# Two modulation sections of layer 1, loaded and multiplied around the low-rank projections of layer 0

## The chip, the cores and the metric

The kernel runs on one core of a Trainium2 chip. The metric is the device time of one execution in microseconds; the time of the kernel before is the median of three runs. Half of a per cent is 5.3 us. A core has TensorE (matrix products, its weight loads overlap them), VectorE (DVE), ScalarE (ACT), GpSimd (POOL) and SyncE (SP), which here issues nearly all weight loads. All inputs lie in HBM, weights as fp32.

## The reference

Two layers of a diffusion trunk over 256 latent tokens (`x`) and 256 context tokens (`xc`), 1024 wide. Each layer derives six modulation rows for either stream from a conditioning vector, with one large weight, mixes tokens, and sends every token to two of 32 experts:

```python
ada = silu(c) @ w_ada[l] + b_ada[l]             # the same for c_ctx; w_ada[l]: 1024 x 6144
sh1, sc1, g1, sh2, sc2, g2 = split(ada, 6)      # sections 0 .. 5
h = x * (1 + sc1) + sh1
p = h @ w_in[l]                                 # q low-rank 384 | kv low-rank 256 + 32 | conv 512 | pool 256
...                                             # latent attention, convolution, pooling, one out projection
x = layer_norm(ALPHA * x + g1 * mix, ln1)
h2 = x * (1 + sc2) + sh2
x = layer_norm(ALPHA * x + g2 * moe(h2), ln2)   # router, then 32 experts of 1024 x 256
```

The modulation of a layer depends on `c` and `c_ctx` alone, so it can be computed at any time before its layer.

## The kernel before

**Loads.** All large weights come through one list, `plan`, in pieces of at most 1 MB. `pump` gives the next piece of the list to the slot that was freed first and issues its load on SP's queue; `done` frees a piece's slot once its last reader has read it. Until layer 0's experts there are six slots (`RING`), so piece n of the list waits until piece n - 6 is used up. Section `sec` of layer `l` is four pieces of 1 MB (`ada_src`); `ink_src` are the two pieces of the weights for kv low-rank and rotary key (called k here), `inq_src` the two of q low-rank, then `ukv` and `uq` (two). The list for layer 0 is: section 1, two column blocks, section 0, one column block, section 2, k, q, ukv, uq, sections 3 to 5, out projection (four), then **sections 1 and 0 of layer 1**, then the experts.

**Modulation.** `ada_mm` (L296) multiplies one piece: 8 matmuls of 32 columns by 256, four side by side in the array; the profile counts each twice, 64 for a section. `ada_add` (L305, L307) copies or adds the result into a row tile on VectorE.

**Mixing of layer 0.** After the column blocks come section 2 and then `lowrank` for k and for q: the weights of two of the eight row blocks (a chunk) are split into a high half (ScalarE, L395) and a remainder (VectorE or POOL, L401) and multiplied with the tokens in three products (L407 to L409, `mm3`). A fixed list gives the first k chunk's remainder to POOL. There are two buffers for split weights. VectorE also runs the taps of a depthwise convolution (L606), which are needed only later. Then follow keys, values and queries from ukv and uq, attention head by head (with the products of sections 3 to 5 between heads), and the out projection.

**Router.** For each of four blocks of 128 tokens: normalise, transpose on TensorE (L1068), copy (ScalarE, L1073), product with the router weights (L1079), result to VectorE (L1081). `fill_ada(n)` multiplies n of the eight pieces of layer 1's sections 1 and 0 between these, by the list `FILL[0]`: 0, 1, 2 and 2 behind the blocks and 6 at the end. Then short VectorE steps choose experts and places; a one-hot product gathers the tokens, and a conditional block for overfull experts follows (L1592). The residual for the next norm is scaled and shifted by rows that are broadcast from HBM (loads L344, POOL L1490, then L1470 and L1471 on VectorE and POOL).

**Experts.** 16 pairs: gate and up products (L1400), the hidden values on VectorE (L1409, L1410), transpose (L1416), down product (L1444) and scatter (L1458). Five more 1 MB slots are free here.

**Order.** Outside the experts, where TensorE's order is as written, a scheduler orders each engine's instructions with a model of their times; what is written first goes first when its inputs are there by that model. On the chip each engine then runs its list in that order.

Of the kernel before, what the change touches and what calls it, by code (L numbers as in the profile page):

```python
# [26 lines left out]
CAP = 64  # L27
NONE = 1024.0
RING = 6
FILL = ((0, 1, 2, 2, 6), (0, 1, 3))  # L30
PA = (0, 1)
VP = (5, 7, 9)
SPG = ((4, 7, 18, 20), (2, 4, 6, 10, 12, 14, 20))
# [14 lines left out]
def trunk(ctx: ExitStack, tc: tile.TileContext, a, out, dbg=None, cap=CAP):  # L48
# [14 lines left out]
    def ada_src(l, sec):  # L63
        w = a["w_ada"][l, :, sec * D:(sec + 1) * D].rearrange("(p j) c -> p j c", j=8)
        for jp in range(4):
            plan.append((("ada", l, sec, jp), w[:, 2 * jp:2 * jp + 2, :], (2, D)))

    def in_src(l, which=(0, 1, 2)):
        w = a["w_in"][l].rearrange("(p j) c -> p j c", j=8)
        for k in which:  # L70
            n, c0 = "agp"[k], (672, 928, 1184)[k]
            plan.append(((n, l), w[:, :, c0:c0 + 256], (8, 256)))

    def inq_src(l):
        w = a["w_in"][l].rearrange("(p j) c -> p j c", j=8)
        for h in range(2):
            plan.append((("q", l, h), w[:, 4 * h:4 * h + 4, 0:384], (4, 384)))

    def ink_src(l):
        w = a["w_in"][l].rearrange("(p j) c -> p j c", j=8)  # L80
        for h in range(2):
            plan.append((("k", l, h), w[:, 4 * h:4 * h + 4, 384:672], (4, 288)))

    def uq_src(l):
        w = a["uq"][l].rearrange("(p j) c -> p j c", j=3)
        for h in range(2):
            plan.append((("uq", l, h), w[:, :, 512 * h:512 * h + 512], (3, 512)))

    def ukv_src(l):
        plan.append((("ukv", l), a["w_ukv"][l].rearrange("(p j) c -> p j c", j=2), (2, 1024)))  # L90

    def out_src(l):
        w = a["w_out"][l].rearrange("(b p) c -> p b c", p=128)
        for hf in range(2):
            for bb in (1, 0):
                plan.append((("out", l, hf, bb), w[:, 4 * bb:4 * bb + 4, 512 * hf:512 * hf + 512], (4, 512)))
# [9 lines left out]
    def exp_src(l):  # L106
        def piece(nm, key, pick):
            plan.append(((nm,) + key, lambda: expert(nm, l, pick), (2, 1024)))

        def pair(nm, i):  # L110
            for e in (2 * i, 2 * i + 1):
                piece(nm, (l, e), lambda w, e=e: w[e:e + 1])

        def picked(nm):
            piece(nm, ("v",), lambda w: w[ds(extra[0], 1)])

        pair("g0", 0)
        for i in range(E // 2):
            pair("g1", i)
            if i + 1 < E // 2:  # L120
                pair("g0", i + 1)
            if i + 2 < E // 2 or (i + 2 == E // 2 and not AHEAD[l]):
                pair("wd", i)
            elif i + 1 == E // 2:
                if AHEAD[l]:
                    pair("wd", i - 1)
                for hf in range(2):
                    n = CUT[l][hf]
                    plan.append((("wd", l, 2 * i + hf), lambda hf=hf, i=i, n=n: [
                        a["w_down"][l, e:e + 1, :, c:c + n].rearrange("o (p j) c -> p (o j) c", j=2)  # L130
                        for c in range(512 * hf, 512 * hf + 512, n) for e in (2 * i, 2 * i + 1)],
                        (1024 // n, 2 * n)))
            if l == L - 1 and i == VP[1]:
                picked("g0")
                picked("g1")
            if l == L - 1 and i == VP[2]:
                picked("wd")

    for l in range(L):
        if l == 0:  # L140
            ada_src(0, 1)
            in_src(0, (0, 1))
            ada_src(0, 0)
            in_src(0, (2,))
        else:
            ada_src(1, 2)
            in_src(1, (0, 1))
            ada_src(1, 3)
            in_src(1, (2,))
        if l == 0:  # L150
            ada_src(0, 2)
        ink_src(l)
        inq_src(l)
        ukv_src(l)
        uq_src(l)
        for key in ((0, 3), (0, 4), (0, 5)) if l == 0 else ((1, 4),):
            ada_src(*key)
        out_src(l)
        for sec in (1, 0) if l == 0 else (5,):
            ada_src(1, sec)  # L160
        exp_src(l)

    if dbg is not None:
# [125 lines left out]
    def ada_mm(l, sec, ps, j0, j1):  # L289
        k = PLACE[sec][1]  # L290
        for jq in range(j0, j1):
            w = get(("ada", l, sec, jq))
            for jj in range(2):
                j = 2 * jq + jj
                for q in range(4):
                    T.matmul(ps[32 * q:32 * q + 32, :256], scw[:, j, 6 - 2 * k:38 - 2 * k],  # L296
                             w[:, jj, q * 256:q * 256 + 256], start=(j == 0), stop=(j == 7),
                             skip_group_check=True, tile_position=(0, 32 * q))
            done(("ada", l, sec, jq))
# [9 lines left out]
    def ada(l, sec, psum):  # L309
        ps = psum()  # L310
        ada_mm(l, sec, ps, 0, 4)
        ada_add(l, sec, ps)
# [54 lines left out]
    def mixing(l, P, norm):  # L367
# [3 lines left out]
        with ExitStack() as cs:  # L371
# [290 lines left out]
            if l:  # L662
                ada_mm(1, 3, ps3, A3, 4)
                ada_add(1, 3, ps3)
            else:
                ada(0, 2, psum)


            def lowrank(nm, toks, width, pss, n0=0, n1=4):
                for n in range(n0, n1):  # L670
                    hh, jq = divmod(n, 2)
                    w = get((nm, l, hh))
                    wh, wl = wsplit(w[:, 2 * jq:2 * jq + 2, :], 2 * width)
                    if jq:
                        done((nm, l, hh))
                    for jj in range(2):
                        j = 4 * hh + 2 * jq + jj
                        for k, t in enumerate(toks):
                            mm3(pss[k][:, :width], hTh[j][:, t * 128:(t + 1) * 128],
                                hTl[j][:, t * 128:(t + 1) * 128], wh[:, jj, :], wl[:, jj, :],  # L680
                                j == 0, j == 7)
                return pss
# [44 lines left out]
            with tc.issue_after(kept_pow[0].ins):  # L727
                conv_part(1, CONV1[l], CONV[l])
            lowrank("q", range(nq), 384, pq_, QS[l], 4)
            cos, sn = rope[:, :, 0:32], rope[:, :, 32:64]  # L730
            tr = t2(FT)[:, 0:128].rearrange("p (a b c) -> p a b c", a=2, b=2)
            kv_ = kr[:, 0:2, :].rearrange("p t (x y r) -> p t x y r", x=2, y=2)
# [317 lines left out]
            lg = per.tile([128, 4, 36], FT, tag="lg", name="lg")  # L1050
            mvs, hTs = [], {}

            todo = [(1, s_, j) for s_ in ((1, 0) if l == 0 else (5,)) for j in range(4)]
            held = {}

            def fill_ada(n):
# [44 lines left out]
            def behind(t):  # L1101

                if t >= 1:
                    merge(t - 1, 1)
                    rows_T(t - 1)
                    stats(t - 1)
                    fill_ada(FILL[l][t - 1])
                if t >= 2:
# [13 lines left out]
            else:  # L1122
# [4 lines left out]
                for t in range(nq):  # L1127
                    fill_ada(FILL[l][t])
                    if t + 1 < nq:
# [26 lines left out]

            fill_ada(FILL[l][-1])
            for t in range(nq):
# [805 lines left out]
```

## Time and profile before

| | |
|---|---|
| median of three runs (1063.36 to 1068.73) | 1065.06 us |
| the profiled execution, its own time | 1073.01 us |
| its span, first to last instruction | 1071.4 us |
| mean granted clock of TensorE | 0.943 |
| TensorE busy | 946.6 us (88%) |
| VectorE busy | 621.0 us (58%) |
| moved by DMA | 305.41 MB, mean 285 GB/s |

The rows of the page and of the trace's views come from the one profiled execution. Times in them are in us from the span's start. In a list in order of time a row has the start, the duration, the engine, the line, the operation, result and inputs, shapes and the number of instructions that are merged; in brackets stands the engine's idle time before it and what ended it. In a row of a stretch each engine has its busy time and, in parentheses, its instructions; the last three numbers are TensorE's granted clock as a share of full speed, the mean busy share of the 16 DMA engines, and GB/s.

### The profile page before, as it was taken

What the parts mean: (1) busy time and instruction counts of PE and PEld (TensorE: products, weight loads), DVE (VectorE), ACT (ScalarE), POOL (GpSimd) and SP (SyncE); (2) the same over time, 40 slices, a digit from 0 to 9 for tenths busy, and PEclk for the clock granted to TensorE, in tenths of its full rate; (3) what the DMA queues carried; (4) which work ended last, traced back from release to release, by engine and by line L of the source; (5) the groups of instructions that cost most, each with busy time, mean ns of one, the idle gap of its engine ahead of it and who ended that gap; (6) DMA issues with size and microseconds to landing.
All of it is one profiled execution on the core that took longest, in us unless ns stands there. A gap on an engine that the chain in (4) does not pass through costs nothing. (4 is left out here: it accounts for less than half of the span.)

```text
span 1071.4 us, 14154 instructions
## 1 busy us (share of the span) xinstructions
PE 946.6 (88%) x5217; PEld 561.0 (52%) x5217; DVE 621.0 (58%) x1169; ACT 312.6 (29%) x614; POOL 327.0 (31%) x284
## 2 busy tenths in 40 slices
PE   4995899999687999999999888988958997999994
PEld 3675786688452445444444587745733443444442
DVE  3499967757854344364333899877572343334336
ACT  2443455632401111111111445543312221222211
POOL 2346520001462333333424533102061222123222
PEclk9896999999888999999999999999769998999997
DMA  9843225866898999999998667356677999999981
GB/s 353 329 148 115 97 81 195 318 150 201 310 329 290 289 401 402 403 390 371 401 385 330 246 227 241 137 208 209 237 240 275 390 380 405 380 399 394 401 302 41
DMA packets 95530, 305.41 MB, mean 285 GB/s; under 512 B 10247, under 2 KB 30727, under 8 KB 87392
## 3 DMA queue, kind: packets, MB, share of 16 engines
q1 hardware_dynamic: 89744, 293.77, 75.1%
q0 software_dynamic: 4272, 6.14, 1.8%
q10 hardware_dynamic: 1440, 4.54, 1.1%
q8 instruction: 43, 0.70, 0.3%
q14 instruction: 31, 0.25, 0.1%
HBM read 309.03 MB, written 4.72 MB: 293 GB/s over the span
## 5 line engine op out<-in xcount | busy, mean ns | idle before, releaser
L1462 POOL TENSOR_TENSOR x<-x,tm 128x512 f32<-128x512 f32 x96 | 122.8, 1297 | 306.0 <-DVE tm L1461 305.6
L1400 PE MATMUL gu<-ring,xt 128*64 128x512 f32 x504 | 171.7, 626 | 0.0
L1400 PE MATMUL gu<-slot,xt 128*64 128x512 f32 x416 | 132.3, 605 | 0.0
L1435 DVE SCALAR_TENSOR_TENSOR O<-d,iw,O 128x512 fp32r<-128x512 f32 x63 | 47.2, 750 | 121.3 <-ACT O L1434 121.2
L1458 PE MATMUL y<-O,gt 128*128 128x512 f32 (+2 forms) x400 | 108.6, 407 | 4.2 <-DVE tm L1461 3.4
L1458 PEld LDWEIGHTS y<-O,gt 128*128 128x128 f32 (+1 forms) x400 | 69.6, 188 | 51.1 <-issue 25.9
L1461 DVE TENSOR_TENSOR tm<-y,lnb 128x512 f32<-128x512 f32 (+1 forms) x102 | 68.7, 677 | 45.8 <-PE y L1458 44.2
L1400 PEld LDWEIGHTS gu<-ring,xt 128*64 128x64 f32 x504 | 49.4, 143 | 67.3 <-issue 63.2
L1444 PE MATMUL d<-ring,ht 128*64 128x512 f32 x264 | 82.7, 597 | 1.0 <-DMA ring<-in_w_down_dram 1.0
L1434 ACT ACTIVATE O<-d,iw 128x512 fp32r<-128x512 f32 x63 | 43.3, 688 | 137.5 <-PE d L1444 136.5
L395 ACT ACTIVATE w<-ring 128x1024 fp32r<-128x1024 f32 (+2 forms) x50 | 47.3, 945 | 97.1 <-PE p L409 73.7
L606 DVE SCALAR_TENSOR_TENSOR c0b<-c0a,hw,c0b 128x256 f32<-128x256 f32 (+1 forms) x105 | 72.8, 739 | 0.5
L1409 DVE SCALAR_TENSOR_TENSOR hd<-th,gu 128x256 f32<-128x256 f32 x32 | 13.5, 421 | 89.3 <-ACT th L1408 89.3
L1400 PEld LDWEIGHTS gu<-slot,xt 128*64 128x64 f32 x416 | 38.3, 139 | 50.1 <-issue 47.6
L401 DVE TENSOR_TENSOR w<-ring,w 128x1024 fp32r<-128x1024 f32 (+2 forms) x40 | 50.2, 1256 | 22.9 <-ACT w L395 22.7
L408 PE MATMUL p<-w,hT 128*128 128x288 f32 (+1 forms) x112 | 39.8, 356 | 18.0 <-DVE w L401 17.9
L1444 PE MATMUL d<-slot,ht 128*64 128x512 f32 x168 | 52.6, 595 | 0.0
L1359 POOL DMA_INDIRECT xg<-h2d,ix x28 | 32.9, 1175 | 51.8 <-DVE ix L1358 23.1
L296 PE MATMUL p<-ring,scw 128*32 128x256 f32 x672 | 44.5, 399 | 1.9 <-DMA ring<-in_w_ada_dram 1.9
L1408 ACT ACTIVATE th<-gu 128x256 f32<-128x256 f32 x32 | 12.3, 385 | 108.9 <-PE gu L1400 108.9
L408 PE MATMUL p<-w,mix 128*128 128x512 f32 x96 | 38.5, 401 | 4.7 <-DVE w L401 4.7
L1444 PEld LDWEIGHTS d<-ring,ht 128*64 128x64 f32 x264 | 24.2, 137 | 34.9 <-issue 32.0
(429 smaller groups left out, 1932.6 us busy)
## 6 DMA issues: line engine op xcount, KB each, us to landing
ring<-in_w_ada_dram SPq DMA_DIRECT2D x46, 1024.0 KB
ring<-in_w_down_dram SPq DMA_DIRECT2D x32, 1024.0 KB
ring<-in_w_gate_dram SPq DMA_DIRECT2D x63, 512.0 KB
ring<-in_w_up_dram SPq DMA_DIRECT2D x63, 512.0 KB
slot<-in_w_gate_dram SPq DMA_DIRECT2D x54, 512.0 KB
slot<-in_w_up_dram SPq DMA_DIRECT2D x54, 512.0 KB
slot<-in_w_down_dram SPq DMA_DIRECT2D x21, 1024.0 KB
ring<-in_w_in_dram SPq DMA_DIRECT2D x6, 1024.0 KB
```

The source lines that it names most:

```text
L296: T.matmul(ps[32 * q:32 * q + 32, :256], scw[:, j, 6 - 2 * k:38 - 2 * k], w[:, jj, q * 256:q * 256 + 256], start=(j == 0), stop=(j == 7), ...
L395: kept_hi.append(S.activation(h_, src, AF.Copy))
L401: ins = e.tensor_tensor(l_, src, h_.bitcast(FT), op=OP.subtract)
L408: T.matmul(ps, lh, rl, start=False, stop=False, skip_group_check=True)
L606: V.scalar_tensor_tensor(acc, tap(b, k), hw[:, b, k:k + 1], acc, op0=OP.mult, op1=OP.add)
L1400: T.matmul(gu[64 * s:64 * s + 64, :].rearrange("p (g c) -> p g c", g=2), xt[h][:, j % 4, o0 + 64 * s:o0 + 64 * s + 64], ws[s].rearrange("p ...
L1434: S.activation(oh, ps, AF.Copy, scale=w)
L1435: V.scalar_tensor_tensor(ol, ps, w, oh.bitcast(FT), op0=OP.mult, op1=OP.subtract)
L1444: T.matmul(ps[64 * s:64 * s + 64, :n], ht[:, k, 64 * s:64 * s + 64], ws(s, k, c, n), start=(k == 0), stop=(k == 1), skip_group_check=True, ...
L1458: T.matmul(ps, GT[key][r, t * 128:(t + 1) * 128], O[key][k][r, c], start=(i == 0 and k == 0), stop=(i == m - 1 and k == 1))
L1461: V.tensor_tensor(tm, ps, gates[t // 2][hf][:, c0:c0 + n], op=OP.mult)
L1462: eng.tensor_tensor(x[:, t, cols], x[:, t, cols], tm, op=OP.add)
```

## The change

The four pieces of section 1 of layer 1 move in the list from behind the out projection to between section 2 of layer 0 and k; those of section 0 to between q and ukv. Their products are written where section 2's are, ahead of the k projection, and behind the q projection. Nothing is left to fill in during layer 0's router: the list `todo` is empty there, and `FILL[0]` is all zeros. Layer 1 keeps its own.

```diff
--- before.py
+++ after.py
@@ -27,7 +27,7 @@
 CAP = 64
 NONE = 1024.0
 RING = 6
-FILL = ((0, 1, 2, 2, 6), (0, 1, 3))
+FILL = ((0, 0, 0, 0, 0), (0, 1, 3))
 PA = (0, 1)
 VP = (5, 7, 9)
 SPG = ((4, 7, 18, 20), (2, 4, 6, 10, 12, 14, 20))
@@ -149,15 +149,18 @@
             in_src(1, (2,))
         if l == 0:
             ada_src(0, 2)
+            ada_src(1, 1)
         ink_src(l)
         inq_src(l)
+        if l == 0:
+            ada_src(1, 0)
         ukv_src(l)
         uq_src(l)
         for key in ((0, 3), (0, 4), (0, 5)) if l == 0 else ((1, 4),):
             ada_src(*key)
         out_src(l)
-        for sec in (1, 0) if l == 0 else (5,):
-            ada_src(1, sec)
+        if l:
+            ada_src(1, 5)
         exp_src(l)
 
     if dbg is not None:
@@ -664,6 +667,7 @@
                 ada_add(1, 3, ps3)
             else:
                 ada(0, 2, psum)
+                ada(1, 1, psum)
 
 
             def lowrank(nm, toks, width, pss, n0=0, n1=4):
@@ -727,6 +731,8 @@
             with tc.issue_after(kept_pow[0].ins):
                 conv_part(1, CONV1[l], CONV[l])
             lowrank("q", range(nq), 384, pq_, QS[l], 4)
+            if l == 0:
+                ada(1, 0, psum)
             cos, sn = rope[:, :, 0:32], rope[:, :, 32:64]
             tr = t2(FT)[:, 0:128].rearrange("p (a b c) -> p a b c", a=2, b=2)
             kv_ = kr[:, 0:2, :].rearrange("p t (x y r) -> p t x y r", x=2, y=2)
@@ -1050,7 +1056,7 @@
             lg = per.tile([128, 4, 36], FT, tag="lg", name="lg")
             mvs, hTs = [], {}
 
-            todo = [(1, s_, j) for s_ in ((1, 0) if l == 0 else (5,)) for j in range(4)]
+            todo = [(1, 5, j) for j in range(4 * l)]
             held = {}
 
             def fill_ada(n):
```

## Rows read from the trace of the kernel before

**Rows 1.** 40 slices of the page, 26.8 us each: TensorE busy, GB/s moved

```profile
PE   4995899999687999999999888988958997999994
...
GB/s 353 329 148 115 97 81 195 318 150 201 310 329 290 289 401 402 403 390 371 401 385 330 246 227 241 137 208 209 237 240 275 390 380 405 380 399 394 401 302 41
```

**Rows 2.** busy time by stretch: engine columns, granted clock, DMA share, GB/s

```profile
80.00:90.00 10.00, 3.14 (x16) 2.90 (x15) 10.00 (x7) 3.86 (x6) 9.69 (x7) 0.65 0.57 215
...
150.00:160.00 10.00, 10.00 (x49) 8.29 (x48) 6.18 (x17) 3.96 (x7) 3.49 (x3) 1.00 0.30 106
```

**Rows 3.** TensorE in order of time: start, duration, line; idle before, releaser

```profile
73.37 3.66 PE L296 MATMUL p<-ring,scw 128*32 128x256 f32 x64
...
87.40 0.61 PE L408 MATMUL p<-w,hT 128*128 128x288 f32 x1 [6.86 <-DVE w L401]
...
98.84 0.61 PE L408 MATMUL p<-w,hT 128*128 128x288 f32 x1 [5.41 <-DVE w L401]
...
134.61 0.73 PE L780 MATMUL p<-t,w 128*128 128x512 f32 x2 [1.21 <-DVE w L401]
```

**Rows 4.** who SP's queue waited for until 420: total, times, longest

```profile
SPq L187 <- PE gu L1400: 21.1, 3, 12.3
```

**Rows 5.** TensorE's waits in the experts of layer 0: total, times, longest

```profile
PE y L1416 <- DMA ring<-in_w_up_dram: 1.3, 1, 1.3
PE d L1444 <- DMA ring<-in_w_down_dram: 1.0, 1, 1.0
```

**Rows 6.** TensorE in order of time, at the end of layer 0's router

```profile
279.08 1.93 PE L296 MATMUL p<-ring,scw 128*32 128x256 f32 x32
280.95 1.98 PE L1079 MATMUL p<-wb,hT 128*128 128x36 f32 x16
```

**Rows 7.** VectorE in order of time, router and first expert pair

```profile
282.96 0.20 DVE L1081 TENSOR_TENSOR lg<-p,sums 128x36 f32<-128x36 f32 x1 [0.97 <-PE p L1079]
...
309.16 1.23 DVE L1343 TENSOR_SCALAR gt<-iot,iw 128x512 fp32r<-128x512 f32 x1
...
310.64 0.48 DVE L1343 TENSOR_SCALAR gt<-iot,iw 128x512 fp32r<-128x512 f32 x1
...
316.53 1.21 DVE L1471 TENSOR_TENSOR x<-x,lnb 128x1024 f32<-128x1024 f32 x1
...
320.08 5.88 DVE L1471 TENSOR_TENSOR x<-x,lnb 128x1024 f32<-128x1024 f32 x1
```

**Rows 8.** ScalarE in order of time, the last token block of the router

```profile
278.61 1.07 ACT L1073 ACTIVATE hT<-p 128x512 f32<-128x512 f32 x2
```

**Rows 9.** SP's DMA issues before the experts of layer 0

```profile
292.51 1.60 SPq L344 DMA_DIRECT2D lnb<-in_rpack_dram  x2
```

**Rows 10.** SP's DMA issues in order of time, around the low-rank projections

```profile
54.68 21.02 SPq L189 DMA_DIRECT2D ring<-in_w_in_dram  x4
76.23 0.34 SPq L189 DMA_DIRECT2D ring<-in_w_ukv_dram  x1
```

**Rows 11.** TensorE's clock and the DMAs' GB/s: idle, then busy again

```profile
80.60:83.00 2.40, 0.00 (x0) 0.99 1.00 406
...
87.40:93.40 6.00, 6.00 (x24) 0.52 0.40 131
```

**Rows 12.** one 1 MB piece alone on the queues (issued at 104.18)

```profile
104.00:109.00 5.00, 4.92 (x34) 4.54 (x33) 4.94 (x9) 4.56 (x16) 0.00 (x0) 1.00 0.60 210
```

**Rows 13.** POOL and ScalarE in order of time: the two halves of a split

```profile
71.90 1.88 POOL L401 TENSOR_TENSOR w<-ring,w 128x576 fp32r<-128x576 f32 x1
...
74.78 0.68 ACT L395 ACTIVATE w<-ring 128x576 fp32r<-128x576 f32 x1
```

**Rows 14.** VectorE in order of time, between the first splits

```profile
85.53 1.81 DVE L401 TENSOR_TENSOR w<-ring,w 128x576 fp32r<-128x576 f32 x1
...
96.98 1.81 DVE L401 TENSOR_TENSOR w<-ring,w 128x576 fp32r<-128x576 f32 x1
```

**Rows 15.** TensorE in order of time, router products of layer 1

```profile
767.13 7.04 PE L1079 MATMUL p<-wb,hT 128*128 128x36 f32 x32
```

## The prediction

> **What bounds the kernel now.** I read the page's 40 slices first, then busy time by stretch where the change takes away and where it adds, then the engines in order of time there. The slices show three stages for layer 0 [rows 1]: token mixing (to about 265 us), the router (to about 295), the experts (to about 590). Within mixing there are two kinds of time. In slices 4 and 5 the DMAs move 97 and 81 GB/s, because the ring is full and its pieces wait to be consumed; this is where the change wants to load. From 80 to 90 us VectorE is busy for all of 10.00 us and TensorE for 3.14; from 150 to 160 it is the other way round, TensorE is full and VectorE has 6.18 [rows 2]. So the low-rank projections (77 to 131 us) wait for VectorE, which runs convolution taps between the weight splits, while everything behind them, to the end of the out projection, is bound by TensorE. What is added to TensorE is free only where it falls in one of the holes before the full stretch: 6.86 us ahead of the second chunk of the k weights, 5.41 us ahead of the third, and 1.21 us ahead of the first key product, each released by a split on VectorE [rows 3].
>
> The moved pieces now stand in front of the expert weights, and the DMAs move about 330 GB/s in slices 10 to 12 [rows 1]. That looks like a bottleneck relieved, but two rows say that it isn't the one which counts. Before the experts get going, SP's queue once waits 12.3 us for TensorE to free a weight buffer [rows 4]: all buffers are full by then, in either kernel. And after that TensorE waits for expert weights 1.3 and 1.0 us in all [rows 5]. Full sooner is still full.
>
> **What is taken away at the router.** Eight pieces of 1 MB and their 64 matmuls, which the profile counts as 128. One section costs 3.66 us [rows 3]. Nearly all of it lies beside other work: the chain there goes over normalisation, transposes, router products and then short VectorE steps. One fill is on the path: 1.93 us of it stands in front of the last token block's router products, and VectorE waits for them until 282.96 [rows 6, 7]. Their input is ready when ScalarE ends its copies, at 278.61 + 1.07 = 279.68 [rows 8], so 280.95 - 279.68 = 1.27 us could go; VectorE waited for only 0.97 of it. I take **-1.0 us**; the bounds are -1.3 and, with the clock (below), +2.1. The two adds of the sections into their rows were made behind the one-hot matrix, beside TensorE's gather: nothing. On SP's queue an expert piece of the same size takes the place of each moved piece, so the row copies that are queued between them wait for the same things: nothing.
>
> With the 8.4 MB gone from the queues, the residual's row broadcasts, issued at 292.51 [rows 9], land sooner, so POOL's scaling of them no longer stands beside VectorE's placement matrices. The first of those took 1.23 us, the second, with the same shape, 0.48 [rows 7]. **-0.75 us**; bounds 0 and -0.75.
>
> **What is added at the low-rank projections.** Section 1 comes ahead of the k weights, both in SP's queue and in TensorE's order. Its own 3.66 us follow the section of layer 0 which ends at 77.03; the hole up to 87.40 covers them [rows 3]. What is less plain is the ring: six slots, filled in plan order. The first piece of the k weights was issued at 54.68, in the slot of a gate weight [rows 10]; now that slot goes to the first moved piece, and the k weights wait for the slot of the third piece of the section that runs at 73.37. In the kernel before, that slot went to the ukv weights, issued at 76.23 [rows 10]. So the k weights are issued **21.5 us later**. Behind this wait stand, on SP's queue, the rest of k, q, the other moved section, ukv and uq.
>
> When do they land? A 1 MB piece alone, issued at 104.18, has moved all its bytes in the stretch that ends at 109, at a mean 210 GB/s over 5 us; the same bytes at the saturated 406 take 2.6 [rows 11, 12], so an estimate from both is some 1.5 us ahead of the first byte. The slots of the last two moved pieces come free when a first and a second quarter of the section at 73.37 are done, the first at 73.37 + 3.66/4 = 74.3. From there two moved pieces and 0.6 MB of k: 74.3 + 1.5 + 2 x 2.6 + 1.5 = 82.5. Then the two halves of a split, 0.68 on ScalarE and 1.88 on POOL [rows 13]: TensorE can do the first chunk at 85.1, not 77.0. That is 8.1 us late, and the clock will be at half by then: the second chunk took 6.00 us at a granted 0.52 after such a pause [rows 11], against 3.5 for the first (77.0 to the start of the first hole, 80.5). The first chunk then ends near 91.1 and the second, at full clock, near 94.6, where it ended at 93.4. The third started at 98.84 in any case, since VectorE made its split only at 96.98 [rows 3, 14]. So if VectorE keeps its order, nothing is lost; the 12.3 us of the two holes cover 3.66 for the section, 85.1 - 80.7 = 4.4 for the wait and 2.5 for the clock, 10.6. If every split moves with the arrival of the k weights, all 8.1 us are lost. The order of VectorE is set by a scheduler, and the trace does not show the new one. I take **+2.0 us**, nearer to the covered end, since VectorE has taps enough to fill either order; bounds 0 and +8.1.
>
> Section 0 comes after the q products. Its pieces wait for slots that k's pieces free, and are there in time. TensorE is full from there on, but the first key product stood 1.21 us waiting for a split [rows 3]: 3.66 - 1.21 = **+2.45 us**; bounds 0 (it is put in the holes) and +3.66. Two small VectorE steps more are hidden by idle time later in mixing [rows 2].
>
> The ukv weights, which were loaded at 76.23, are now issued when the q weights free their slot. Only the split behind the q products reads them, so there is cover; if it were gone, a load of 4 us would show. I book nothing. From the next sections on, each piece waits for the same slot as before.
>
> **The sum.** -1.0 - 0.75 + 2.0 + 2.45 = +2.7 us. The profiled execution took 1073.01 us, so 1075.7 for one like it. It lies 7.95 us above the median of the runs, 1065.06; the median then comes to **1067.8**.
>
> **The rivals.**
> - Slower: the load is late and stays late. The k weights' later issue carries through every split, since VectorE's taps are put in front of them. For it: the late slot is certain, and a hole released by VectorE can't be filled by TensorE's work alone. Against it: VectorE's total work is unchanged. It decides as soon as the third split ends later than 98.84. Price: 8.1 + 3.66 - 1.75 = +10.0, a median of 1075.1.
> - The fills held the clock. Without them the router's TensorE work comes in short bursts between waits. In layer 1, with few fills, 32 router products took 7.04 us, or 0.22 each [rows 15], where 16 take 1.98 here, or 0.124 [rows 6]. The last two blocks stand back to back once the fill between them is gone: 2 x 16 x (0.22 - 0.124) = 3.1 us more, +2.1 in place of -1.0, a sum of +5.8 and a median of 1070.9. The Trainium skill, "TensorE: Matmul & The Clock Gate", section "A second HAM failure mode: psum-queue depth-cycling", speaks for it: short idle times between groups of matmuls are enough to let the clock swing between its levels; layer 1's 0.22 us agrees, and no row shows it yet for layer 0.
> - Faster: the holes take both sections, and a stall at the experts' start opens. VectorE's residual step at 320.08 took 5.88 us where the same step at 316.53 took 1.21, since POOL runs its own beside it; the first expert pair's hidden values wait behind it [rows 7]. Moved a little against POOL, it gives back 4.7: -1.75 - 4.7 = -6.4, a median of 1058.6.
> - The queues were the bound after all: 8.4 MB at 406 GB/s [rows 11] are 20.7 us, a median near 1044. Rows 4 and 5 speak against it.
>
> **How the numbers follow.** Forecast 0.47, late load 0.20, clock 0.15, faster 0.15, queues 0.03. Half a per cent, 5.3 us, is about what a measurement of this kernel can tell from no change. The forecast's own range is 1064 to 1072, with 0.36 of it within half a per cent, 0.10 slower and 0.01 faster. The late load is slower with 0.17 and within with 0.03; the clock is split 0.08 within, 0.07 slower; the faster rival is 0.09 faster and 0.06 within. So: faster 0.13, same 0.53, slower 0.34. The range is 1057 to 1077: it takes in both bounds of the k weights' delay and the residual's stall, and leaves out the queues.
>
> **What would show it.** Right: section 1's matmuls directly behind 77 us, the first k chunk near 85 at half clock, the third split near where it was, and the out projection ending some 4 us later. The last router products then come up to 1 us sooner against the out projection's end. Wrong: a third k chunk past 103 (late load), router products at 0.2 us each (clock), a residual step that no longer takes 5.88 us (faster), or expert weights that TensorE waits for no more and experts that end much sooner (queues).

## The result, and the profile after

| | before | after |
|---|---|---|
| median of the runs | 1066.89 us (1063.36 to 1068.99, 4) | 1080.97 us (1078.97 to 1081.62, 4) |
| the profiled execution, its own time | 1073.01 us | 1081.62 us |
| its span; mean granted clock | 1071.4 us; 0.943 | 1079.9 us; 0.939 |

The change makes the kernel slower: the ratio of after to before is 1.0124, with an interval of 1.0076 to 1.0171. The forecast was 1067.8 us in 1057 to 1077, "same" the likeliest; the time is 13.2 us above the forecast and 4 us outside the range. All ratios here leave out executions in a slower state, of which there was one, 2033.21 us among the ten of e11_all_res.

**Where the two profiled executions part.** Each number is the end of a step in us from the span's start; differences are those of the rounded numbers:

| end of | before | after | after - before | added in the step |
|---|---|---|---|---|
| q products | 130.8 | 136.2 | 5.4 | 5.4 |
| out projection | 265.1 | 273.0 | 7.9 | 2.5 |
| last router logits (their start on VectorE) | 283.0 | 292.9 | 9.9 | 2.0 |
| placement (start of the token gather) | 295.1 | 308.0 | 12.9 | 3.0 |
| first pair's hidden values | 326.3 | 339.9 | 13.6 | 0.7 |
| last pair of layer 0 (its first transposes) | 583.4 | 595.3 | 11.9 | -1.7 |
| layer 1, last work of TensorE | 1058.5 | 1067.1 | 8.6 | -3.3 |

The medians lie 14.1 us apart, these two executions 8.6. The profiled execution of before is a bad one: at 1073.01 it lies above all four of its runs. Two of its steps are longer than in other executions. One is the step to the first hidden values (e4_before below). The other is layer 1's router, where TensorE's clock differs: its 32 products, 7.04 us in before [rows 15], take 4.10 in after:

```profile
777.88 4.10 PE L1085 MATMUL p<-wb,hT 128*128 128x36 f32 x32
```

That isn't the change's doing. Of the fourteen profiles in this document five have these products at 7.04 us (before, e4, e2, e7, e11) and nine at 3.76 to 4.39, whether a section was moved or not.

**Low-rank projections.** TensorE of after in order of time: start, duration, line, operation; in brackets the idle time before and what ended it.

```profile
79.06 1.07 PE L299 MATMUL p<-ring,scw 128*32 128x256 f32 x16 [0.77 <-DMA ring<-in_w_ada_dram]
...
82.82 1.93 PE L299 MATMUL p<-ring,scw 128*32 128x256 f32 x16 [2.69 <-DMA ring<-in_w_ada_dram]
...
85.24 1.33 PE L410 MATMUL p<-w,hT 128*128 128x288 f32 x4 [0.49 <-ACT w L398]
87.24 0.61 PE L411 MATMUL p<-w,hT 128*128 128x288 f32 x1 [0.67 <-POOL w L404]
...
99.49 0.61 PE L411 MATMUL p<-w,hT 128*128 128x288 f32 x1 [7.24 <-DVE w L404]
...
136.18 3.66 PE L299 MATMUL p<-ring,scw 128*32 128x256 f32 x64
```

Section 1 itself waits for its pieces (0.77 and 2.69 us), and the k weights come last: the first chunk starts at 85.24 with the products of its high half, and goes on with those of its remainder at 87.24, behind POOL's split. The remainder of the second waits until 99.49 for a split on VectorE; before it waited until 87.40 [rows 3]. Section 0 takes its 3.66 us at 136.18. ScalarE's first splits in after, and VectorE's taps and splits:

```profile
84.50 1.26 ACT L398 ACTIVATE w<-ring 128x576 fp32r<-128x576 f32 x2 [10.13 <-issue]
```

```profile
81.49 6.25 DVE L609 SCALAR_TENSOR_TENSOR c0b<-c0a,hw,c0b 128x512 f32<-128x512 f32 x6
...
87.99 5.38 DVE L609 SCALAR_TENSOR_TENSOR c0b<-c0a,hw,c0b 128x512 f32<-128x512 f32 x8
...
93.63 4.08 DVE L609 SCALAR_TENSOR_TENSOR c0b<-c0a,hw,c0b 128x512 f32<-128x512 f32 x3
97.63 1.81 DVE L404 TENSOR_TENSOR w<-ring,w 128x576 fp32r<-128x576 f32 x1
...
103.04 0.74 DVE L404 TENSOR_TENSOR w<-ring,w 128x576 fp32r<-128x576 f32 x1
```

VectorE's first split stands at 97.63, where in before it stood at 85.53 and the next at 96.98 [rows 14]. The weights were there sooner: ScalarE had split its half of the first two chunks by 85.76. What stands ahead of VectorE's split is its own order, with 17 convolution taps from 81.49 on, which nobody waits for yet. Of its 45 taps VectorE does 28 before its first split here and in e9_sec1, and 13 in before, e1, e4 and e6 below, in which the k weights keep their slot.

**Router.** TensorE of after, and its clock (the number before the DMA share) in stretches of 10 us:

```profile
279.24 1.97 PE L1074 MATMUL p<-ident,x 128*128 128x128 f32 x8 [2.78 <-ACT x L1105]
281.00 3.46 PE L1085 MATMUL p<-wb,hT 128*128 128x36 f32 x16
284.27 1.95 PE L1074 MATMUL p<-ident,x 128*128 128x128 f32 x8
286.01 6.88 PE L1085 MATMUL p<-wb,hT 128*128 128x36 f32 x32
```

```profile
270.00:280.00 10.00, 7.22 (x50) 6.60 (x49) 9.49 (x20) 5.68 (x7) 5.38 (x6) 0.97 0.43 157
280.00:290.00 10.00, 10.00 (x50) 10.00 (x48) 6.02 (x12) 7.79 (x8) 2.58 (x2) 0.50 0.29 102
290.00:300.00 10.00, 2.89 (x14) 2.77 (x14) 8.47 (x16) 3.73 (x3) 5.00 (x2) 0.50 0.54 161
300.00:310.00 10.00, 2.52 (x23) 2.44 (x23) 9.62 (x18) 0.20 (x1) 7.43 (x8) 0.50 0.00 0
```

The last 32 router products take 6.88 us, 0.215 each, where before 16 took 1.98 [rows 6]. The granted clock is 1.2 GHz (0.50) from about 280 on, though TensorE is busy for all of 10.00 us in 280 to 290. It fell behind 2.78 us of idle time, in the place of one fill.

**Placement.** SP, POOL and VectorE of after:

```profile
287.13 1.01 SPq L347 DMA_DIRECT2D lnb<-in_rpack_dram  x2
```

```profile
295.00 2.78 POOL L1496 TENSOR_SCALAR lnb<-lnb 128x1024 f32<-128x1024 f32 x1 [12.42 <-DMA lnb<-in_rpack_dram]
297.76 2.87 POOL L1161 TENSOR_TENSOR h<-hn,h 128x1024 fp32r<-128x1024 f32 x1
300.60 2.78 POOL L1496 TENSOR_SCALAR lnb<-lnb 128x1024 f32<-128x1024 f32 x1
...
303.95 2.84 POOL L1161 TENSOR_TENSOR h<-hn,h 128x1024 fp32r<-128x1024 f32 x1
```

```profile
297.84 2.92 DVE L1247 TENSOR_SCALAR t<-t 128x32 f32<-128x32 f32 x2
...
303.94 3.92 DVE L1237 TENSOR_TENSOR g<-iot,pos 128x1024 fp32r<-128x1024 f32 x1
```

POOL of before:

```profile
306.33 5.69 POOL L1490 TENSOR_SCALAR lnb<-lnb 128x1024 f32<-128x1024 f32 x2 [6.64 <-DMA lnb<-in_rpack_dram]
```

The residual's row broadcasts are issued at 287.13 instead of 292.51 [rows 9], and land at 295.00 instead of 306.33. So POOL scales them inside the chain that chooses experts and places, and its own part of the tokens (L1161) is pushed back beside VectorE's steps. Two steps of 32 elements take VectorE 2.92 us together (0.26 in e3 below, where the scaling is elsewhere). The placement matrix takes 3.92 (1.21 in e11), but 3.71 in e3 too: that isn't the scaling's, and in both it stands beside POOL's L1161.

**The first expert pair.** VectorE and POOL of after:

```profile
333.19 6.38 DVE L1477 TENSOR_TENSOR x<-x,lnb 128x1024 f32<-128x1024 f32 x1
339.49 0.41 DVE L1416 TENSOR_TENSOR hd<-hd,gu 128x256 f32<-128x256 f32 x1
```

```profile
333.84 2.35 POOL L1477 TENSOR_TENSOR x<-x,lnb 128x1024 f32<-128x1024 f32 x1
336.13 2.34 POOL L1476 TENSOR_TENSOR x<-x,lnb 128x1024 f32<-128x1024 f32 x1
```

The residual step that took 5.88 us before [rows 7] takes 6.38. It starts 0.65 us ahead of POOL's step, lasts through two of POOL's, and ends 1.1 us after the second (338.47), about its own length.

### The profile page after: what moved, and what is told of

Read it like the earlier page. It is cut to its first block, busy times and chain, and to the rows that moved or that the text cites. A ratio compares the mean times of both kernels' runs of the same rounds, so it can differ in the third digit from the quotient of the medians.

```text
span 1079.9 us, 14158 instructions
## 1 busy us (share of the span) xinstructions
PE 943.5 (87%) x5217; PEld 563.4 (52%) x5217; DVE 626.0 (58%) x1169; ACT 312.8 (29%) x614; POOL 326.7 (30%) x284
## 5 line engine op out<-in xcount | busy, mean ns | idle before, releaser
L1406 PE MATMUL gu<-ring,xt 128*64 128x512 f32 x504 | 167.1, 609 | 0.0
L404 DVE TENSOR_TENSOR w<-ring,w 128x1024 fp32r<-128x1024 f32 (+2 forms) x40 | 49.1, 1230 | 26.8 <-ACT w L398 26.5
L1365 POOL DMA_INDIRECT xg<-h2d,ix x28 | 33.6, 1200 | 53.3 <-DVE ix L1364 25.5
```

The costliest lines, as they stand in the source:

```text
L404: ins = e.tensor_tensor(l_, src, h_.bitcast(FT), op=OP.subtract)
L1406: T.matmul(gu[64 * s:64 * s + 64, :].rearrange("p (g c) -> p g c", g=2), xt[h][:, j % 4, o0 + 64 * s:o0 + 64 * s + 64], ws[s].rearrange("p ...
```

## The experiments

"Out projection" is the end of that stage; "router and placement" goes from there to the token gather, "first pair" from the gather to the first hidden values, all in the profiled execution. The ratio is that of the timed runs to those of the kernel before on the same chip, with its interval; it isn't the quotient of two medians. The medians of before that go with the ratios are 1066.89 us (after), 1066.08 (e1 to e3), 1063.79 (e6 to e9) and 1066.40 (e10 to e13).

| kernel | out projection | router and placement | first pair | sum | median us | ratio |
|---|---|---|---|---|---|---|
| before | 265.1 | 30.0 | 31.2 | 326.3 | | |
| e4_before | 262.3 | 33.3 | 26.7 | 322.3 | 1068.84 (one) | |
| after | 273.0 | 35.0 | 31.9 | 339.9 | 1080.97 | 1.0124 [1.0076, 1.0171] |
| e1_k_first | 269.6 | 35.2 | 31.6 | 336.4 | 1078.53 | 1.0138 [1.0095, 1.0181] |
| e2_fill | 272.2 | 36.6 | 31.2 | 340.0 | 1082.42 | 1.0167 [1.0125, 1.0209] |
| e3_late | 273.2 | 32.0 | 31.7 | 336.9 | 1080.12 | 1.0146 [1.0095, 1.0198] |
| e9_sec1 | 270.2 | 30.8 | 31.0 | 332.0 | 1077.04 | 1.0135 [1.0104, 1.0166] |
| e6_sec0 | 266.2 | 30.1 | 31.7 | 328.0 | 1070.29 | 1.0068 [1.0039, 1.0097] |
| e7_fill_end | 264.6 | 36.0 | 33.9 | 334.5 | 1078.38 | 1.0126 [1.0088, 1.0163] |
| e8_residual | 264.4 | 33.3 | 25.5 | 323.2 | 1064.35 | 0.9999 [0.9971, 1.0027] |
| e10_after_res | 271.9 | 34.8 | 25.0 | 331.7 | 1076.7 | 1.0115 [1.008, 1.0149] |
| e11_all_res | 268.8 | 30.0 | 23.9 | 322.7 | 1070.33 | 1.0034 [1.0005, 1.0063] |
| e12_fill2_res | 262.1 | 29.9 | 25.2 | 317.2 | 1061.35 | 0.9970 [0.9949, 0.9990] |
| e13_end_res | 264.5 | 36.3 | 23.3 | 324.1 | 1068.16 | 1.0030 [1.0001, 1.0059] |

**Theory and rivals.** Four costs were suspected from the traces: the late k weights with section 1's own time, section 0's time, the clock in the router, and the early broadcasts. The first kernels take them singly.

**e1_k_first**: the k weights keep their slot, section 1 follows the k products.

```diff
+        ink_src(l)
+        if l == 0:
             ada_src(1, 1)
-        ink_src(l)
...
-                ada(1, 1, psum)
...
+            if l == 0:
+                ada(1, 1, psum)
             pq_ = [psum() for _ in range(nq)]
```

> The changed kernel with the k weights ahead of section 1 in the list, and the k products ahead of section 1's. Theory (late load: the k weights wait for a slot until 76 us, and every later split moves with them): the first k chunk is back at 77 us, the q products end near 131 to 135 where they ended at 136.2, and the run is 4 to 6 us faster than the changed kernel, near 1076. Rival (what was lost is TensorE's time for 128 more matmuls, whatever the load does): within 2 us of the changed kernel, and the q products end near 136 again.

The k products start at 76.2 and the out projection ends at 269.6. Six profiles with before's mixing stage (before, e4, e7, e8, e12, e13) end it at 262.1 to 265.1, 263.8 in the mean; four with after's (after, e2, e3, e10) at 271.9 to 273.2, 272.6 in the mean; e1 and e11 at 269.2. So the two moves cost 8.8 us here, and 3.4 of it (272.6 - 269.2) is the late load, with section 1's place ahead of k. VectorE's first split is back at 84.77, and the q products end at 133.0, as expected. In the time, the 3 us can't be told: 1078.53 where 1076 was expected.

**e2_fill**: dummy matmuls, whose result nothing uses, stand where the fills were. **e3_late**: POOL scales the broadcasts only behind the router's last POOL step.

```diff
-                    fill_ada(FILL[l][t])
+                    fill_dummy((0, 1, 2, 2)[t])
...
+            fill_dummy(3)
```

```diff
-                    G.tensor_scalar(t_, t_, ALPHA, None, op0=OP.mult)
+                    with tc.issue_after(marks["info"].ins):
+                        G.tensor_scalar(t_, t_, ALPHA, None, op0=OP.mult)
```

> The changed kernel with matmuls of the same shape on resident data in the router, as many and at the places where the kernel before had its pieces; they load nothing and their result is not used. Theory (the fills held the clock): granted clock 1.0 through the router products, 0.12 us each, the last logits 10.0 - 2.1 = 8 us later than before instead of 10, the run 2 to 5 us faster than the changed kernel, near 1077. Rival (the clock falls because the queues or the order of other engines changed): router products stay at 0.21 us, and the run is 0 to 3 us slower for the extra matmuls.

> The changed kernel with POOL's scaling of the residual's broadcast rows put behind the routing information in POOL's order, where the kernel before had it because the rows came late. Theory (the early broadcast let POOL take VectorE's port in the router's chain): from the last logits to the first gather 12.2 us as before, where the changed kernel took 15.1, and the run 2 to 3 us faster than the changed kernel, near 1078.5. Rival (VectorE is slowed by the casts it shares with POOL in either kernel): still about 15 us, no faster.

TensorE of e2, the last block of the router:

```profile
288.00 1.98 PE L1094 MATMUL p<-wb,hT 128*128 128x36 f32 x16
```

Matmuls that compute nothing of use bring the clock back: 16 products take 1.98 us, 0.124 each, and the last logits come 17.8 us after the out projection, as in before (17.9), where after takes 19.9. So it is the clock, and not the queues or a late input, that makes after's router slow. But e2's placement takes 18.8 us instead of 15.1, for POOL's scaling now stands elsewhere in its chain, at 4.55 us:

```profile
293.78 4.55 POOL L1509 TENSOR_SCALAR lnb<-lnb 128x1024 f32<-128x1024 f32 x1 [11.97 <-DMA h2d<-hn]
```

```profile
304.14 0.39 DVE L1259 TENSOR_REDUCE t<-t 128x4 f32<-128x32 f32 x2 [7.15 <-POOL t L1258]
```

VectorE waits 7.15 us for a small step that POOL has queued behind it. e3 takes the scaling out: the placement falls from 15.1 to 12.0 us, before's 12.1. Each is worth 2 to 3 us in its stage; neither shows in the time, whose intervals are wider (1077 and 1078.5 us were expected).

**e4_before**: the kernel before, profiled once more.

> The kernel before, profiled once more, to see where its executions differ: its profiled one took 1073.01 us, its others 1063.4 to 1069.0. Theory (its layer 1 is what varies): the same marks to the end of layer 0's experts within 1 us, layer 1 some 4 to 6 us shorter. Rival (layer 0 varies): the first expert pair's hidden values at another time than 326.3.

It shows what varies without any change. The theory missed: layer 1 takes 475.4 us here and 475.2 in the first profile. Layer 0 varies, with the first hidden values at 322.3 instead of 326.3. TensorE, then VectorE and POOL:

```profile
268.55 1.16 PE L1068 MATMUL p<-ident,x 128*128 128x128 f32 x8 [1.38 <-ACT x L1099]
269.55 2.59 PE L1079 MATMUL p<-wb,hT 128*128 128x36 f32 x16
272.07 3.64 PE L296 MATMUL p<-ring,scw 128*32 128x256 f32 x30
```

```profile
320.77 1.21 DVE L1471 TENSOR_TENSOR x<-x,lnb 128x1024 f32<-128x1024 f32 x1
```

```profile
322.88 2.37 POOL L1471 TENSOR_TENSOR x<-x,lnb 128x1024 f32<-128x1024 f32 x1
```

The clock falls behind an idle time of 1.38 us and the fill takes 3.64 us, twice its time, so that the last logits come 22.3 us after the out projection; but the residual step takes 1.21 us instead of 5.88, since POOL's comes 2.1 us later. In before, then, the stall that the forecast took for a fixed part of either kernel is there in some executions only. This gave the fifth suspect: the changed kernel stalls always. All six profiles that have a section moved and this order as it was (after, e1, e2, e3, e6, e9) take 6.37 or 6.38 us in this step. What they share shows one step earlier. POOL of after, then of before:

```profile
330.37 1.48 POOL L1365 DMA_INDIRECT xg<-h2d,ix  x1 [1.96 <-DVE ix L1364]
```

```profile
317.50 1.42 POOL L1359 DMA_INDIRECT xg<-h2d,ix  x1 [0.19 <-POOL xg L1727]
```

In all six POOL has waited 1.96 us for VectorE's `ix`. Both engines run on from that one step, and VectorE's residual step starts 0.65 us ahead of POOL's each time. In before POOL comes behind its own memset, and the lead is whatever that leaves: 0.16 us in the first profile, 2.11 in e4.

**e9_sec1** and **e6_sec0** move one section each; the other stays as fill, one quarter of it behind each block.

```diff
-FILL = ((0, 1, 2, 2, 6), (0, 1, 3))
+FILL = ((0, 1, 1, 1, 1), (0, 1, 3))
...
```

> The kernel before with only section 1 moved ahead of the k weights; section 0 stays as fill of the router (one piece's quarter per block, FILL 0,1,1,1,1). Theory now: the late k weights and section 1's own 3.66 us are not covered by the holes, so the out projection ends 5 to 6 us later than before (265.1 us in the profiled execution before); the router chain behind it, 17.9 us from there to the last logits, stays near 18, since the fills hold the clock; the lnb broadcasts land later than in the changed kernel. Time: before + 5 to 6. Prediction on record, by its terms: + 2.0 at the low-rank projections, so before + 2 or less.

> The kernel before with only section 0 moved behind the q products; section 1 stays as fill of the router (FILL 0,1,1,1,1). The k weights keep their slot and are issued as before. Theory and prediction agree: 3.66 us of matmuls less the 1.21 us hole that they fill, so the out projection ends 2.45 us later, and the time is before + 2.4; with the router's fills kept, no part of the rise is there. Rival: section 0's four pieces delay ukv and uq, and the out projection ends 5 us or more later.

In the stage they add up: section 0 costs 266.2 - 263.8 = 2.4 us, section 1 ahead of k 270.2 - 263.8 = 6.4, together the 8.8 of the change. Each is one profile, and before's own six lie 3 us apart, so that they add up so well is partly luck. Of section 1's 6.4, 3.4 are the late load (e1) and 3.0 its own time. In these two profiles three quarters between the blocks instead of five are enough for the clock: the last logits come 17.2 us after the out projection in both. The times say more than the stage. Section 0 alone costs 7 us, 1.0068, where 2.4 were expected; the first pair explains it, at 31.7 us with a stall of 6.38. Section 1 alone costs as much as the whole change, 1.0135, where 5 to 6 us were expected. The stall, which is there too, accounts for 4 or 5 us of it, and several us stay open: the profile is the fastest of its four executions (1072.68 us at a granted clock of 0.953; the others took 1076.5 to 1080.6 at 0.938 to 0.945). The two alone make more than both together, in part since either brings the whole stall.

**e7_fill_end** moves no load at all: the fills stand behind the router.

```diff
-FILL = ((0, 1, 2, 2, 6), (0, 1, 3))
+FILL = ((0, 0, 0, 0, 8), (0, 1, 3))
```

> The kernel before with both sections left where they are, but all eight quarters behind the last router products instead of between the blocks. It asks for the clock alone, with no load moved. Clock theory: the router products of the last blocks take 0.2 us each at a granted clock near 0.5, and the time from the out projection's end to the last logits is 19.9 us as in the changed kernel, against 17.9 before: before + 2 at the logits. Rival (the changed kernel's slow router comes from something else, its late start or its empty queues): the clock stays and the last logits come 1.0 us sooner. What follows to the experts' first pair is as before in both, unless the eight quarters of 0.9 us delay the gather.

```profile
270.91 1.97 PE L1068 MATMUL p<-ident,x 128*128 128x128 f32 x8 [2.79 <-ACT x L1099]
272.68 3.46 PE L1079 MATMUL p<-wb,hT 128*128 128x36 f32 x16
...
277.69 5.17 PE L1079 MATMUL p<-wb,hT 128*128 128x36 f32 x24
```

The same rows as in after: 2.79 us idle, then 3.46 us for 16 products. The chain to the last logits takes 21.1 us, for a few matmuls of the fill still stand ahead of the last eight products. + 2 was expected at the logits and nothing behind them; the time is 1.0126, as much as the whole change. It isn't the clock alone: the row broadcasts are issued sooner here too, and POOL scales them from 287.00 on, where it did from 306.33. The router and the placement make 3 to 6 us of the time (36.0 against 30.0 to 33.3). Much of the rest is the first pair (33.9 us), where VectorE stalls again:

```profile
324.67 6.35 DVE L1471 TENSOR_TENSOR x<-x,lnb 128x1024 f32<-128x1024 f32 x1
```

**e8_residual** and **e10_after_res** take the stall away in before and in after, **e13_end_res** in e7: VectorE's residual steps are issued behind the first pair's hidden values.

```diff
-                    e.tensor_tensor(xs, xs, r_[0], op=OP.mult)
-                    e.tensor_tensor(xs, xs, r_[1], op=OP.add)
+                    with tc.issue_after(kept["last"].ins) if e is V and "last" in kept else nullcontext():
+                        e.tensor_tensor(xs, xs, r_[0], op=OP.mult)
+                        e.tensor_tensor(xs, xs, r_[1], op=OP.add)
```

> The kernel before with one order changed: VectorE's residual steps of layer 0's expert stage are issued only behind the hidden values of the first expert pair. It tests the stall of up to 5.88 us that stands ahead of these hidden values in the kernels before and after. Theory (VectorE's step, made beside POOL's own, holds the first pair's hidden values and so all pairs): the first pair is 4 to 5 us sooner, time before - 4. Rival (POOL's steps slow whatever VectorE does there, or the expert weights end the wait next): within 1 us of before.

> The changed kernel with one order changed: VectorE's residual steps of layer 0's expert stage are issued only behind the hidden values of the first expert pair, as in e8_residual, where the same edit to the kernel before was worth nothing in the time. Theory: in the changed kernel the stall (6.38 us for a step of 1.21) is there in every execution, since VectorE's last step comes just ahead of POOL's; in the kernel before it is there in some only. Then the stretch from the gather to the first hidden values goes from 31.9 to near 26, and the time falls by 5, to before + 9. Rival (the stall is no more the rule after the change than before): no change in the time, before + 14.

> The kernel before with all eight quarters behind the last router products, as in e7_fill_end (before + 14), and with the residual steps behind the first hidden values. Theory: what e7 lost is the clock in the router and the placement, about 4 us and some for the quarters at half clock, and 5 to 7 at the residual stall, which now goes: before + 7 to 8. Rival (the clock alone makes e7's loss): before + 13 as in e7.

e10, then e13, VectorE:

```profile
331.31 0.42 DVE L1416 TENSOR_TENSOR hd<-hd,gu 128x256 f32<-128x256 f32 x1
331.65 6.08 DVE L1477 TENSOR_TENSOR x<-x,lnb 128x1024 f32<-128x1024 f32 x1
```

```profile
323.67 0.42 DVE L1410 TENSOR_TENSOR hd<-hd,gu 128x256 f32<-128x256 f32 x1
324.00 8.50 DVE L1471 TENSOR_TENSOR x<-x,lnb 128x1024 f32<-128x1024 f32 x2
```

The long steps are still there, but behind the hidden values, where nothing waits for them. In before the edit is worth nothing in the time (0.9999): its theory, - 4, missed. In e7 it is worth 10 us: 1.0126 becomes 1.0030, and the intervals don't meet; 7 to 8 us over before were expected, and 3 are left. In after the first pair falls from 31.9 to 25.0 us, but the time doesn't tell: the medians' excess over before goes from 14.1 to 10.3 us, the ratio only from 1.0124 to 1.0115, and the intervals overlap. So the cost of the stall is shown in the time for e7, and for after in the stage alone, with 7 us. That before mostly lacks the stall fits with e8, which gains nothing, and with e4; it is argued, not shown.

**e11_all_res** undoes all but the sections' own matmul time.

> The changed kernel with everything undone but the two sections' own time on TensorE: section 1 behind the k products with the k weights first in the queue, dummy matmuls in the router in the place of the fills (their result goes to a scratch row that nothing reads), POOL's scaling of the row broadcasts behind the router's info, and the residual steps behind the first hidden values. Theory: 3.4 us for section 1 and 2.1 for section 0 remain at the low-rank projections, the router and the placement take about 30 us, the first pair 26: before + 5. Rival (something else in the change still costs, the expert weights' early load say): before + 9 or more.

```profile
284.63 1.98 PE L1096 MATMUL p<-wb,hT 128*128 128x36 f32 x16
```

```profile
297.44 1.21 DVE L1249 TENSOR_TENSOR g<-iot,pos 128x1024 fp32r<-128x1024 f32 x1
```

Router products take 0.124 us again and the placement matrix 1.21. Router and placement come to 30.0 us, the first pair to 23.9, and the excess falls to 3.6 us (0.34% of 1066.4), near the 5 that were expected: the 5 us left at the low-rank projections, less what the first pair gains. So nothing else in the change costs much, the earlier loads of the expert weights included.

**e12_fill2_res** gives before one more quarter where TensorE stood idle for 1.38 us, with the residual order of e8.

```diff
-FILL = ((0, 1, 2, 2, 6), (0, 1, 3))
+FILL = ((0, 2, 2, 2, 6), (0, 1, 3))
```

> The kernel before with the residual steps behind the first hidden values and with two quarters of a section instead of one between the first and the second token block of the router (FILL 0,2,2,2,6), where TensorE stood idle for 1.39 us and where the clock fell in two of three profiles. Theory: the clock holds and the router chain is 17.9 us in each execution instead of 22.4 in some: before - 2 to - 3. Rival (the fill's second quarter delays the second block's transposes, or the clock falls anyway): before to before + 1.

```profile
268.39 1.16 PE L1068 MATMUL p<-ident,x 128*128 128x128 f32 x8 [0.95 <-ACT x L1099]
269.39 1.87 PE L1079 MATMUL p<-wb,hT 128*128 128x36 f32 x16
```

The idle time shrinks to 0.95 us, the next products take 1.87 where e4 took 2.59, and the chain to the last logits 17.8 us where e4 and e8 took 22.3 and 22.4. At 1061.35 us and a ratio of 0.9970 [0.9949, 0.9990] this kernel beats the one before by about 3 us, as expected: with more fill between the blocks, not less. The interval of e8, which has the residual order alone, overlaps its own (0.9971 to 1.0027), so that the extra quarter is what gains is likely, not shown. That the clock holds in each execution rests on one profile and a narrower spread (1059.01 to 1064.06).

## Why the prediction was wrong

**Right: what bounds what.** The queues were not the bound. SP's longest wait for a weight buffer is there in after too, and TensorE still waits for one expert piece:

```profile
SPq L190 <- PE gu L1406: 20.1, 3, 14.4
```

```profile
PE y L1422 <- DMA slot<-in_w_up_dram: 1.3, 1, 1.3
```

From the fourth pair's first transposes to the last pair's it takes 206.1 us against 205.8: 8.4 MB less in front of the experts bring nothing there [rows 4, 5]. Section 0 behind q was forecast at + 2.45 and costs 2.4 against the mean of before's six profiles, 1.1 to 4.1 against single ones. The k weights were issued at 75.71, 21.0 us later than before's 54.68, where 21.5 was forecast. The first k chunk was forecast for 85.1 and starts at 85.24, partly by luck: its splits, forecast for 82.5 to 85.1, run from 84.50 to 87.18, and it starts on the high half alone.

**The failed term at the projections: + 2.0 for section 1.** It was worked out as if VectorE kept its order, so that the holes cover the section, the wait and the clock; the bound of + 8.1 held the other case. VectorE's order moved with the load: the first of its splits came at 97.63 instead of 85.53 [rows 14], behind 15 more taps, though the weights were there by 85.76; the third chunk's split ended at 103.78 instead of 98.79. Section 1 cost 6.4 us, 3.4 for the late load and 3.0 for the section's own 3.66. That is the late-load rival, which had 0.20, though not at its full price of + 10.0: the k products end 4.3 us later, not 8.1. A hole that another engine releases covers added work only if that engine's order stays, and this one was free to change.

**The failed term at the router: - 1.0 for the fill.** The rival "the fills held the clock" is what the two profiled executions show: forecast + 2.1, measured + 2.0 at the last logits, with 0.215 us per product where 0.22 was forecast. In the median its size stays open. In after, e1, e3 and e10 the chain takes 19.8 to 20.0 us, but in before's order not always 17.9: in e4 and e8 the clock falls with the fills in place, the fills themselves slow down, and the chain is 22.3 and 22.4. The Trainium skill ("TensorE: Matmul & The Clock Gate", "A second HAM failure mode: psum-queue depth-cycling") says that frequent short idle times between groups of matmuls let the clock swing. The runs agree that short idle times do it: it fell at an idle time of 2.78 us in after and of 2.79 in e7; of the profiles with 1.38 to 1.41 us it fell in e4 and e8 and stood in before, e2 and e11. The forecast put the rival at 0.15 with layer 1 in sight, where few fills stand and a product takes 0.22 [rows 15]. That row was worth more weight, but less than it seems: in after the same products take 0.13 us (4.10 for 32). Where the fill is short but the clock holds (e6, e9), the chain is 17.2 us, 0.7 shorter: the - 1.0 had its mechanism right.

**The failed term at the broadcasts: - 0.75.** It was asked what their earlier landing would free, not what it would meet. POOL's 5.6 us of scaling (2 x 2.78) went from beside the steps of [rows 7] into the placement's chain: + 3.0, undone by e3. The gain itself didn't come either: the first of the two matrices took 2.01 us in after, where it had taken 1.23.

**The failed assumption at the stall.** The forecast had it in both kernels at 5.88 us, from the one execution that was profiled [rows 7], and gave its end to the faster rival (0.15). It was the other way round: one of two profiles of before lacks it, taking it away gains before nothing in the time, and all six profiles with a section moved have it. The profiled execution stood 7.95 us above its median, which the forecast noted and then subtracted as a constant. That gap was the sign that some of its rows were not the median's.

**The sum, term by term.** The projections cost 8.8 us in the mean of the profiles (4.45 forecast). Against the first profile of before, router and placement cost 5.0 (- 1.75 forecast), the first pair 0.7 (0 forecast) and the pairs behind it - 1.7: 12.8 in all. Against e4, which has no stall but a slow clock in the router, these are 1.7, 5.2 and - 1.3: 14.4. The time says 14.1 by the medians and 13.2 by the ratio. Layer 1 is left out, as the slow value of its router is in both profiles of before and not in after's (471.8 us for the layer against 475.2 and 475.4); how often before has it isn't known, so the division of the 14 us among the terms is good to some 4 us.

**The clock rival and the late-load rival came together.** They were priced as cases of which one holds. Their causes are independent parts of one change, and both at once would have been + 10.0 + 3.1 = + 13.1, a median of 1078.2, outside the range given. That it lies near the result is partly chance, since the terms differ: 8.8 and not 11.8 at the projections, + 3.0 and not - 0.75 at the broadcasts, and the stall on top.

## What to carry to other kernels

Matmuls that look like filler between short dependent steps can be what keeps TensorE's clock up; before they are moved, look at the products around them and at a stage that lacks them, in more than one execution. When a load or an order moves, ask of every engine's queue what now starts earlier and beside what, not only what is freed. And where the profiled execution lies well above the median, take a second look at the same kernel before a stall in it is booked as fixed.

## What the runs showed of the hardware

The stall on VectorE was larger than expected, and one-sided. A step of 1.21 us that starts 0.65 us ahead of POOL's ended only after two of POOL's steps, 6.38 us later, while these took 2.35 and 2.34; one that starts 2.1 us ahead took its 1.21. The Trainium skill ("SBUF — State Buffer", "Who interferes with whom") says that a VectorE instruction with two inputs in SBUF contends with a GpSimd instruction that reads SBUF, and that the shared ports are an exclusive lock. The waiting agrees; that a step of VectorE lasts through two instructions of POOL in a row, and starts first in the profile, is what these rows add. And once the clock had fallen behind 2.78 us of idle time, it stayed at 0.50 from 280 to 310 in after, though the row has TensorE busy for 10.00 us of the first ten; in e2, with matmuls between the blocks, the router's products kept their 0.124 us.
